# The short set's mLSTM as full-length scores: one round for each query chunk in place of a chunk recurrence in two directions

## The chip, the cores and the metric

One NeuronCore of a Trainium2 chip runs the whole program. The metric is the device time of one execution in microseconds; the kernel before takes 2311.3 us, the median of three runs (2310.19 to 2314.37).

## The reference

One encoder layer runs on two token sets with the same weights: `x_prompt` with 1024 tokens (set A, "long") and `x_sample` with 512 tokens (set B, "short"), 1024 channels each. After a norm and one big input projection there are two branches, an mLSTM in both directions (4 heads of 256) and a dilated attention (3 groups of 8 heads of 64); both are gated, projected and merged. The change touches the mLSTM of the short set. In one direction the reference computes, chunk by chunk of 128 positions,

```python
bc = jnp.cumsum(fc, axis=-1)
d_log = jnp.where(tril, bc[..., :, None] - bc[..., None, :] + ic[..., None, :], -jnp.inf)
a = bc + m[..., None]
mt = jnp.maximum(a, jnp.max(d_log, axis=-1))
sc = jnp.einsum('nhtk,nhsk->nhts', qc, kc) * jnp.exp(d_log - mt[..., None])
wa = jnp.exp(a - mt)
num = jnp.einsum('nhts,nhsv->nhtv', sc, vc) + wa[..., None] * jnp.einsum('nhtk,nhkv->nhtv', qc, c_mat)
den = jnp.sum(sc, axis=-1) + wa * jnp.einsum('nhtk,nhk->nht', qc, n_vec)
h = num / jnp.maximum(jnp.abs(den), jnp.exp(-mt))[..., None]
...
c_new = decay[..., None, None] * c_mat + jnp.einsum('nhsk,nhsv->nhkv', kw, vc)
```

and then sums both directions and normalises each head. Without chunks the same `h_t` is a sum over all earlier positions s of `(q_t . k_s) * exp(u_s - M_t) * v_s`, where `u` is the input gate less the running sum `bc` of log forget gates and `M_t` the running maximum of `u` (at least 0); the divisor is the larger of the weights' own sum in absolute value and `exp(-(bc_t + M_t))`.

## The kernel before, in words

TensorE's and SP's instructions stand in the order in which the program is written (`manual_schedule`); for VectorE, ScalarE and GpSimd a scheduler sets the order. Every product that must be exact runs as three passes over pieces split in two (`mm3`, lines L193 to L195: high x high, high x low, low x high); plain 128x128 products of unsplit numbers appear twice each in the records.

After the long set's input projection the program is a row of stages, each made of small dependent steps with dense work strewn between: the long set's scans (`mlstm(A)`), its attention (`attend(A)`), the short set's scans (`mlstm(B)`), its attention, the ends. The dense work is the `Fill` object's list of units: `fill.stage(steps, shares)` spreads a fixed number of steps over the stage (`STEPS`, 194 for the short set's scans), and `fill(1/3)` issues what is due. A step is three 512-wide products in a row (`dense`). Weights for them come by `wraw` DMAs (L241) and are split by ScalarE (L249) and VectorE (L250); a unit's end is written out by ScalarE and VectorE (L713, L714). Beside the short set's scans runs `combine(A)`, the mixing of the long set's attention groups, one piece after each half round: VectorE mostly (L1412 to L1419), with a turn on TensorE (L1424).

The gates: `gates_of` puts the gate columns into the tile `gall`, and `lanes` (L841 to L926) turns them so that head, direction and chunk are lanes, scans along 128 positions (L870, L873), carries the maximum across chunks, and writes the rows `rw` and the columns `col`. For the short set this runs in pieces beside `attend(A)`.

`mlstm` has a round for each head, chunk and direction: 32 for the short set. Once a head, `prepare` makes k.q for equal chunks (L987) and turns k (L996) with ScalarE copies (L989, L997). `front(k)`, one round ahead, masks and exponentiates the row (L1019, L1021), multiplies it with the scores (L1022), splits it into `sch` and `scl` (L1025, L1026), weights and splits q (L1030 to L1034) and k (L1040, L1041). `core(k)` then issues the products: scores by v into the PSUM tile `num`, k by v into `kv`, q by the carried state `C` into `num`; updates and splits the state (L1072 to L1079); and divides (L1082 to L1086, L1089). In the second half of a head's rounds the two directions meet, and the chain to `hn` follows: square and sum (L1091), a root on GpSimd (L1092, L1093), scaling (L1094). Three rounds later `turn` transposes `hn` into an `a` tile (L1101), VectorE multiplies the gate (L1103) and SP stores it. PSUM holds two banks of `a`, two of `num`, two of `kv`, and two of the dense work.

Of the kernel before, what the change touches and what calls it, by code (L numbers as in the profile page):

```python
# [37 lines left out]
EPS = 1e-6  # L38
NEG = -1e30
# [32 lines left out]
class Tokens:  # L72


    def __init__(self, dram, S, x, y, name):
        self.S, self.x, self.y, self.n, self.nblk, self.name = S, x, y, S // P, S // BLK, name
        t = lambda shape, what, dt=F32: dram.tile(shape, dt, name=f"{what}_{name}")
        self.qk = t([16, P, S], "qk")
        self.vs = t([2, S, D], "vs")
        self.G = t([8, P, S], "G")  # L80
        self.aqk = t([2, 24, P, S], "aqk")
        self.av = t([S, 1536], "av")
        self.az = t([4, P, S], "az")
        self.gt = t([2, 8, P, S], "gt")
        self.rw = t([8, self.n, 2, P], "rw")
        self.ym = t([12, P, S], "ym")
        self.og = t([3, 4, S, OW], "og")

# [88 lines left out]
class Net:  # L177
# [651 lines left out]

    def gates_of(self, T, t):  # L830

        return T.gall.rearrange("p (j r) -> p j r", r=32)[:, :, :4 * T.n].rearrange("p j (h c) -> p j h c", c=T.n)[:, :, :, t]

    def gate_tile(self, T, pool):
        T.gall = pool.tile([P, P], F32, name=f"gall{T.S}")
        self.nc.gpsimd.memset(T.gall, 0.0)
        T.col = pool.tile([P, 3, 64], F32, name=f"col{T.S}")
        T.gb = pool.tile([P, 1], F32, name=f"gb{T.S}")
        self.nc.sync.dma_start(T.gb, self.a[f"gb{T.n}"])

    def lanes(self, T, sb, bank):  # L841

# [109 lines left out]
    def mlstm(self, T, fill, steps, first, banks, lead, after, beside=()):  # L952
# [10 lines left out]
        with ExitStack() as stack:  # L963
# [184 lines left out]
                next(beside, None)  # L1148
            self.flush(lambda p: True)


    def att_load(self, T, u):

# [474 lines left out]
STEPS = (310, 232, 194, 290, 86)  # L1628


def body(tc, a):
    N = Net(tc, a)
    nc = tc.nc
    (x1, y1), (x2, y2) = a["runs"]
    with ExitStack() as st:
        st.enter_context(tc.manual_schedule(engines={mybir.EngineType.PE}))
        pool = lambda name, bufs, **kw: st.enter_context(tc.tile_pool(name=name, bufs=bufs, side="left", **kw))
# [3 lines left out]
        B = Tokens(dram, 512, a[x2], a[y2], "b")  # L1641
# [5 lines left out]
        ps = N.pool(sps, "ps", 8, "left", PSUM)  # L1647
        with ExitStack() as s1:
# [128 lines left out]
        with ExitStack() as s1:  # L1777
            s1.enter_context(tc.manual_schedule(engines={mybir.EngineType.PE, mybir.EngineType.SP}))
            N.defer = True
            ring = N.pool(s1, "ring", 1, "left")  # L1780
            N.wraw = [ring.tile([P, RING], F32, name=f"wraw{i}") for i in range(2)]
            N.wsplit = [[ring.tile([P, RING], F32R, name=f"w{x}{i}") for x in "hl"] for i in range(3)]
            N.arena = N.pool(s1, "arena", 1, "left")
            N.gate_tile(B, N.pool(s1, "gates", 1, "left"))
            short = N.short_units(B)
            N.last = (B, 0)
            finals = [N.final(*x) for x in ((A, 0), (A, 1), (B, 0))]
            units = short[:-4] + N.branches(A, 0, 0, short[-4:])
# [12 lines left out]
            keep.close()  # L1801
            kept = {}

            def hold(name, make):
                def go():
                    kept[name] = make()
                return go

            with ExitStack() as s2:
                sp = N.pool(s1, "sp", 1, "right")  # L1810
                N.sw = Rot(N, [sp.tile([P, BLK], F32R, name=f"sw{i}") for i in range(4)])
                sraw = sp.tile([P, BLK + 2], F32R, name="sraw")
                N.sg, N.sraw = Rot(N, [sraw[:, :BLK]]), sraw.bitcast(F32)
                N.mlstm(A, fill, STEPS[0], N.ml_load(A, 0), ("a", "num", "kv"), 4,
                        hold("qkv", lambda: N.att_load(A, 0)))
                with ExitStack() as s3:
                    lanes = N.lanes(B, N.pool(s3, "lane2", 1, "right"), lambda: N.bank("o").rearrange("p a b -> p (a b)"))
# [24 lines left out]
            end = N.pool(s1, "end", 1, "right")  # L1842
            N.xo_bufs.insert(0, ("late", [end.tile([P, BLK], F32, name=f"xo2{i}") for i in range(2)]))
            with ExitStack() as s2:
                cmb_ps = N.pool(s2, "cmb_ps", 2, "right", PSUM)
                azs = [end.tile([P, BLK], F32, name=f"az{i}") for i in range(2)]
                mixed = N.combine(B, lambda: cmb_ps.tile([P, 4, P], F32, name="tp2"), ("V0a", "V1a"),
                                  ("X1", "Q0"), N.osb, azs, False)
                next(mixed)
                fill.stage(STEPS[4], 3 * B.n + 6)  # L1850
                fill(4)
                for _ in mixed:
                    N.tick()
                    fill(1)
                N.flush(lambda p: True)
            while fill.step():
                if fill.done % 8 == 0:
                    N.tick()
            N.flush(lambda p: True)


def _layout(i):

    f = lambda n: np.asarray(i[n])
    w = f("w_in")[0]
# [13 lines left out]
    def gate_bias(n):  # L1879
        o = np.zeros((4, 32), np.float32)  # L1880
        o[:, :4 * n] = np.repeat(gb, n, axis=1)
        return o.reshape(P, 1)
# [9 lines left out]
        "gb8": gate_bias(8), "gb4": gate_bias(4),  # L1892
# [22 lines left out]
```

## Time and profile before

| What | Value |
|---|---|
| Time, median of 3 runs | 2311.3 us |
| Span of the profiled execution | 2308.8 us |
| TensorE busy | 2261.8 us (98%) |
| VectorE, ScalarE, GpSimd busy | 1493.6, 1134.9, 663.0 us |
| Mean DMA rate | 181 GB/s |
| Mean granted TensorE clock | 0.995 |

The profiled execution is one of its own: its span, from the first instruction to the last, is 2.5 us below the median time. In rows of instructions, `out<-in` gives the tiles, then partitions x elements, a count, the busy time in us and the mean of one in ns, and the idle time ahead with what ended it. In rows of the timeline the start and the length are in us, and the idle time ahead stands in brackets. TensorE's records overlap, so the pace is read from the starts of neighbours.

### The profile page before, as it was taken

The numbers are of one execution on the slowest core, as the hardware profiler recorded it, in microseconds if no ns is written. First come the engines' busy times: TensorE is split into PE (matmuls) and PEld (weight loads), VectorE is DVE, ScalarE is ACT, GpSimd is POOL, SyncE is SP. The second block draws the span as 40 slices with busy tenths as digits, with TensorE's granted clock in tenths as the row PEclk, the third lists the DMA queues.
The fourth block names the chain that finished last, engine by engine and source line by source line (L and its number), as shares of the span: only waits on it lengthen the run. The fifth ranks groups of instructions, "written<-read, shape, count | busy, mean of one in ns | idle before, by whom it ended". The sixth has DMA issues, their size and how long they took to land.

```text
span 2308.8 us, 36431 instructions
## 1 busy us (share of the span) xinstructions
PE 2261.8 (98%) x12610; PEld 1977.8 (86%) x12610; DVE 1493.6 (65%) x2905; ACT 1134.9 (49%) x2375; POOL 663.0 (29%) x888
## 2 busy tenths in 40 slices
PE   8999999999999999999999999999999999999998
PEld 8999888888788888889999889998878788888787
DVE  7765577689886654466777756665488844555563
ACT  6332243434444443366667656766666544544432
POOL 2000333333332232135556500011144321421321
PEclk9999999999999999999999999999999999999999
DMA  3652455542222243294674689887678778686673
GB/s 120 169 127 74 171 207 193 192 171 103 108 104 86 84 151 114 78 331 129 217 241 146 189 219 234 230 237 207 190 252 252 216 229 242 198 254 208 214 257 113
DMA packets 253170, 418.85 MB, mean 181 GB/s; under 512 B 25177, under 2 KB 150297, under 8 KB 252986
## 3 DMA queue, kind: packets, MB, share of 16 engines
q1 hardware_dynamic: 249384, 403.93, 55.9%
q10 hardware_dynamic: 3602, 12.59, 1.4%
q8 instruction: 100, 1.64, 0.3%
q14 instruction: 84, 0.69, 0.1%
HBM read 296.44 MB, written 128.39 MB: 184 GB/s over the span
## 4 chain that ended last, share of the span: by engine, by line
PE 78%; DMA 8%; DVE 5%; issue 5%; ACT 2%; SPq 1%; POOL 1%; DVEq 0%; POOLq 0%; ACTq 0%
PE d L195 11%; PE d L193 11%; PE d L194 11%; PE dense L193 10%; PE dense L195 10%; PE dense L194 10%; PE o L1296 3%; PE pt L1284 2%; PE lg L1261 2%; PE num L193 1%; DVE pwk L678 1%; PE num L195 1%; PE num L194 1%; DMA vs_a<-vz 1%; DMA Q<-aqk_b 1%
## 5 line engine op out<-in xcount | busy, mean ns | idle before, releaser
L193 PE MATMUL dense<-H,wh 128*128 128x512 f32 x672 | 279.5, 416 | 1.4 <-DVE sw L714 1.4
L195 PE MATMUL dense<-H,wl 128*128 128x512 f32 x672 | 265.7, 395 | 0.0
L194 PE MATMUL dense<-H,wh 128*128 128x512 f32 x672 | 265.5, 395 | 0.0
L195 PE MATMUL d<-Hh,phla 128*128 128x512 f32 x608 | 237.1, 390 | 3.8 <-DVE phla L610 3.8
L193 PE MATMUL d<-Hh,phla 128*128 128x512 f32 x608 | 236.6, 389 | 0.0
L194 PE MATMUL d<-Hl,phla 128*128 128x512 f32 x608 | 236.5, 389 | 0.0
L250 DVE TENSOR_TENSOR wl<-wraw,wh 128x1024 fp32r<-128x1024 f32 (+1 forms) x130 | 163.0, 1254 | 98.2 <-ACT wh L249 96.5
L1273 DVE CUSTOM_DVE_ANT_0 ls<-lg,bias 128x256 f32<-128x256 f32 (+1 forms) x288 | 93.7, 362 | 145.6 <-PE lg L1261 55.9
L1277 ACT ACTIVATE ls<-ls,nm 128x256 f32<-128x256 f32 (+1 forms) x288 | 130.0, 453 | 97.6 <-DVE nm L1275 79.4
L195 PE MATMUL d<-Hh,phlb 128*128 128x512 f32 x456 | 177.4, 389 | 0.0
L193 PE MATMUL d<-Hh,phlb 128*128 128x512 f32 x456 | 177.4, 389 | 0.0
L194 PE MATMUL d<-Hl,phlb 128*128 128x512 f32 x456 | 177.4, 389 | 0.0
L249 ACT ACTIVATE wh<-wraw 128x1024 fp32r<-128x1024 f32 (+1 forms) x130 | 137.0, 1054 | 80.1 <-PE dense L194 41.4
L628 POOL TENSOR_TENSOR psum_w<-pw_raw 128x512 f32<-128x512 f32 x38 | 59.2, 1557 | 376.2 <-DMA pw_raw<-w_in 353.0
L195 PEld LDWEIGHTS dense<-H,wl 128*128 128x128 f32 x672 | 127.7, 190 | 29.0
L193 PEld LDWEIGHTS dense<-H,wh 128*128 128x128 f32 x672 | 128.2, 191 | 18.3 <-issue 1.8
L194 PEld LDWEIGHTS dense<-H,wh 128*128 128x128 f32 x672 | 128.5, 191 | 16.6
L193 PE MATMUL d<-vhi,Hh 128*128 128x322 f32 x448 | 141.1, 315 | 1.3 <-ACT Hh L353 1.1
L194 PE MATMUL d<-vlo,Hh 128*128 128x322 f32 x448 | 139.8, 312 | 2.2 <-DVE vlo L427 2.2
L195 PE MATMUL d<-vhi,Hl 128*128 128x322 f32 x448 | 140.3, 313 | 0.4 <-DVE Hl L354 0.2
L195 PEld LDWEIGHTS d<-Hh,phla 128*128 128x128 f32 x608 | 114.1, 188 | 29.4 <-DVE phla L610 5.9
L194 PEld LDWEIGHTS d<-Hl,phla 128*128 128x128 f32 x608 | 114.1, 188 | 23.8
(552 smaller groups left out, 6206.9 us busy)
## 6 DMA issues: line engine op xcount, KB each, us to landing
pw_raw<-w_in SPq DMA_DIRECT2D x76, 512.0 KB
wraw<-w_in SPq DMA_DIRECT2D x76, 512.0 KB
aqk_a<-pwk SPq DMA_DIRECT2D x48, 512.0 KB
aqk_b<-sw SPq DMA_DIRECT2D x48, 256.0 KB
wraw<-w_pm SPq DMA_DIRECT2D x24, 512.0 KB
wraw<-w_out SPq DMA_DIRECT2D x24, 512.0 KB
wraw<-w_v SPq DMA_DIRECT2D x18, 512.0 KB
erep<-erow SPq DMA_DIRECT2D x16, 512.0 KB
```

Source lines behind the costliest of these rows:

```text
L193: nc.tensor.matmul(out, lh, rh, start=start, stop=False)
L194: nc.tensor.matmul(out, lh, rl, start=False, stop=False)
L195: nc.tensor.matmul(out, ll, rh, start=False, stop=stop)
L249: self.splits = (nc.scalar.activation(hi[:, :n], raw[:, :n], AF.Copy), nc.vector.tensor_sub(lo[:, :n], raw[:, :n], hi[:, :n].bitcast(F32)))
L250: nc.vector.tensor_sub(lo[:, :n], raw[:, :n], hi[:, :n].bitcast(F32)))
L628: self.nc.gpsimd.tensor_add(s[:, 0], ws[1][:, 0], ws[1][:, 1])
L678: nc.vector.scalar_tensor_tensor(y, raw[:, i:i + S], cw[:, i:i + 1], y, op0=OP.mult, op1=OP.add)
L1261: nc.tensor.matmul(lg[:, hh, c:c + w], q[hh][:, qs], z[:, k0:k0 + w], start=z is k[hh], stop=z is not k[hh])
L1273: nc.vector.tensor_tensor_reduce(out=ls[:, hh], in0=ts["lg"][hh], in1=bt[:, hh], scale=1.0, scalar=NEG, op0=OP.add, op1=OP.max, accum_out= ...
L1277: nc.scalar.activation(ls[:, hh], ls[:, hh], AF.Exp, bias=nm[:, hh:hh + 1], accum_out=ot[:, 128 + hh:129 + hh])
L1284: nc.tensor.transpose(pp[:, hh * nk + x], ts["ls"][:, hh, x * P:(x + 1) * P], self.ident)
L1296: nc.tensor.matmul(po[:, hh * 64:hh * 64 + 64], pt[:, hh * nk + x], v[:, kt[x], c0 + hh * 64:c0 + hh * 64 + 64], start=x == 0, stop=x == n ...
```

## The change

For the short set alone (512 tokens) there are a new `lanes_short` and a new `mlstm_short`.

- `gall` holds the four chunks apart (128 x 4 x 128), so that a lane is a head and direction alone and a scan runs along all 512 positions (L1181, L1185). No maximum is carried across chunks. It writes one row of maxima for each lane to `rw` and, by four transposes, the columns `u` and `exp(-(bc + M))` to `col`.
- `mlstm_short` has 16 rounds, one for each head and query chunk i. `weigh(k)` makes the weights for both directions in one tile of five blocks: the i+1 blocks of key chunks 0 to i for the forward one, the 4-i blocks of chunks i to 3 for the backward one. VectorE subtracts the row of maxima from the columns (two instructions), GpSimd masks the two diagonal blocks, ScalarE takes the exponential.
- `front(k)` makes the scores of query chunk i with all four key chunks (eight 128x128 products, L1262), VectorE multiplies the weights with them (L1264, L1265), ScalarE and GpSimd split the result (L1268, L1269).
- `core(k, d)` adds up the scores by v over the direction's blocks in one `num` bank and divides; the second direction adds to the first, and the chain to `hn` follows. `turn` comes one round later. There is no `kv`, no state and no turned k; `num` has four banks. The buffer of G is doubled, the rows are fetched once a head and direction.
- The number of dense steps in the stage stays 194. The scratch of DMAs issued by GpSimd goes to 1024 bytes.

```diff
+        for q, o in ((0, li), (64, lf)):
+            nc.scalar.activation(o[0:32], p[q:q + 32], AF.Identity, bias=T.gb[q:q + 32])
...
+        nc.vector.tensor_tensor_scan(bc, one, lf, 0.0, op0=OP.mult, op1=OP.add)
+        yield
+        nc.vector.tensor_sub(u, li, bc)
+        nc.gpsimd.memset(one, 0.0)
+        nc.vector.tensor_tensor_scan(cm, one, u, 0.0, op0=OP.add, op1=OP.max)
+        nc.vector.tensor_add(bc, bc, cm)
...
+            bank = {"a": lambda: ps.tile([P, 4, P], F32, name="a"),
+                    "num": lambda: ps.tile([P, 512], F32, name="num", bufs=4)}
...
+            def weigh(k):
+                h, i = rounds[k]
+                w = made[k] = sb.tile([P, n + 1, P], F32, name="rm")
+                for d in range(2):
+                    b0, c0, m = (0, 0, i + 1) if d == 0 else (i + 1, i, n - i)
+                    u = T.col[:, c0:c0 + m, 32 * d + h]
+                    row = ms[h, d][:, i * P:(i + 1) * P]
+                    nc.vector.tensor_tensor(w[:, b0:b0 + m], u[:, :, None].to_broadcast([P, m, P]),
+                                            row[:, None, :].to_broadcast([P, m, P]), op=OP.subtract)
+                    sg = 1 if d == 0 else -1
+                    nc.gpsimd.affine_select(out=w[:, i + d], in_=w[:, i + d], pattern=[[sg, P]], compare_op=OP.is_ge, fill=NEG,
+                                            base=0, channel_multiplier=-sg)
+                nc.scalar.activation(w, w, AF.Exp)
+
+            def front(k):
...
+                p = psum("a")
+                for j in range(n):
+                    for ct in range(2):
+                        nc.tensor.matmul(p[:, j], kk[:, ct, j * P:(j + 1) * P], q[:, ct, i * P:(i + 1) * P], start=ct == 0,
+                                         stop=ct == 1)
+                nc.vector.tensor_mul(w[:, :i + 1], w[:, :i + 1], p[:, :i + 1])
+                nc.vector.tensor_mul(w[:, i + 1:], w[:, i + 1:], p[:, i:])
...
+                nc.scalar.activation(sch, w, AF.Copy)
+                nc.gpsimd.tensor_sub(scl, w, sch.bitcast(F32))
...
+            def core(k, d):
...
+                js = list(range(i + 1) if d == 0 else range(i, n))
+                pn = psum("num")
+                for j in js:
+                    self.mm3(pn[:, :258], (sch[:, j + d], scl[:, j + d]), (v[0][:, j], v[1][:, j]), j == js[0], j == js[-1])
...
+                if k + 1 < len(rounds):
+                    front(k + 1)
+                if k + 2 < len(rounds):
+                    weigh(k + 2)
+                fill(2 / 3)
+                core(k, 0)
+                fill(1 / 3)
+                next(beside, None)
+                self.tick()
+                turns.pop(k - 1, lambda: None)()
+                fill(2 / 3)
+                core(k, 1)
+                fill(1 / 3)
+                next(beside, None)
...
-                    N.mlstm(B, fill, STEPS[2], kept["head"], ("kv", "num", "a"), 1,
+                    N.mlstm_short(B, fill, STEPS[2], kept["head"], ("num", "a"), 1,
...
-    nc = _bacc.Bacc("TRN2", target_bir_lowering=False, num_devices=1)
+    nc = _bacc.Bacc("TRN2", target_bir_lowering=False, num_devices=1, dynamic_dma_scratch_size=1024)
```

How the order changes. TensorE in a round of the short set's scans before: the state's product, dense work, then q by the carried state (`ch`, `cl` are its split halves).

```order
L195 MATMUL kv<-V1a,kl 128x258
L193 MATMUL dense<-H_7784,wh_7757 128x512
L194 MATMUL dense<-H_7785,wh_7757 128x512
L195 MATMUL dense<-H_7784,wl_7758 128x512
L193 MATMUL num<-ch_17672,qh 128x258
L194 MATMUL num<-cl_17673,qh 128x258
L195 MATMUL num<-ch_17672,ql 128x258
```

TensorE now, where a round begins: one group of eight score products into an `a` bank, then dense work.

```order
L1262 MATMUL a<-Q_17374 128x128 x8
L193 MATMUL dense<-H_7784,wh_7755 128x512
L194 MATMUL dense<-H_7785,wh_7755 128x512
L195 MATMUL dense<-H_7784,wl_7756 128x512
L193 MATMUL dense<-H_7786,wh_7755 128x512
L194 MATMUL dense<-H_7787,wh_7755 128x512
L195 MATMUL dense<-H_7786,wl_7756 128x512
```

The `kv` and `num<-ch` products are gone from the short set's stage, and the score group stands once a round instead of once a head. VectorE before, in the same stage (`cf`, `cl`: the state and its low half; `kl`: the weighted k; `cw`, `az`: the combine; `sw`, `wl`: dense work):

```order
L1426 TENSOR_TENSOR az_16697<-a,az_16697 128x512
L1084 RECIPROCAL r<-r 128x1
L1079 TENSOR_TENSOR cl_17755<-cf_17422,ch_17754 128x516
L1089 SCALAR_TENSOR_TENSOR X_16719<-num,r,X_16719 128x256
L1041 SCALAR_TENSOR_TENSOR kl<-Q_17439,col_7767,kh 128x256
L250 TENSOR_TENSOR wl_7756<-wraw_7752,wh_7755 128x1024
L1394 TENSOR_TENSOR cw_17855<-V1b 128x8
L1075 SCALAR_TENSOR_TENSOR cf_17501<-cf_17501,rw_16712,kv 128x516
L714 SCALAR_TENSOR_TENSOR sw_7867<-dense,sw_7866 128x128x4
L1022 TENSOR_TENSOR rm<-rm,st_16707 128x128
```

VectorE now, with the weights of a later round (L1246), the combine's sums (L1620, L1621), a division (L1285 to L1291) and the product with the scores (L1264, L1265):

```order
L1246 TENSOR_TENSOR rm<-col_7767,rw_16681 128x512
L1246 TENSOR_TENSOR rm<-col_7767,rw_16682 128x128
L250 TENSOR_TENSOR wl_7758<-wraw_7752,wh_7757 128x1024
L1620 TENSOR_TENSOR K_16720<-K_16720 128x512
L714 SCALAR_TENSOR_TENSOR sw_7867<-dense,sw_7866 128x128x4
L1285 TENSOR_SCALAR r<-num,col_7767 128x1
L1621 TENSOR_TENSOR K_16720<-K_16720 128x512
L1286 SCALAR_TENSOR_TENSOR r<-num,r 128x1
L1287 RECIPROCAL r<-r 128x1
L1291 SCALAR_TENSOR_TENSOR hs<-num,r,hs 128x256
L1264 TENSOR_TENSOR rm<-rm,a 128x384
L1265 TENSOR_TENSOR rm<-rm,a 128x256
```

The four state and k instructions have left the row, and the subtraction and the product of five blocks have come in; the division still stands behind the same combine and dense rows.

More of the change, by code (lines that the diff above doesn't have):

```diff
@@ L84, in __init__ @@
         self.gt = t([2, 8, P, S], "gt")
-        self.rw = t([8, self.n, 2, P], "rw")
+        self.rw = t([8, S] if S == BLK else [8, self.n, 2, P], "rw")
         self.ym = t([12, P, S], "ym")
@@ L830, in gates_of @@
     def gates_of(self, T, t):
+        if T.S == BLK:
+            return T.gall[:, t].rearrange("p (j r) -> p j r", r=32)[:, :, :4]
         return T.gall.rearrange("p (j r) -> p j r", r=32)[:, :, :4 * T.n].rearrange("p j (h c) -> p j h c", c=T.n)[:, :, :, t]
     def gate_tile(self, T, pool):
-        T.gall = pool.tile([P, P], F32, name=f"gall{T.S}")
+        short = T.S == BLK
+        T.gall = pool.tile([P, 4, P] if short else [P, P], F32, name=f"gall{T.S}")
         self.nc.gpsimd.memset(T.gall, 0.0)
-        T.col = pool.tile([P, 3, 64], F32, name=f"col{T.S}")
+        T.col = pool.tile([P, 4, P] if short else [P, 3, 64], F32, name=f"col{T.S}")
         T.gb = pool.tile([P, 1], F32, name=f"gb{T.S}")
-        self.nc.sync.dma_start(T.gb, self.a[f"gb{T.n}"])
+        self.nc.sync.dma_start(T.gb, self.a["gb1" if short else f"gb{T.n}"])
     def lanes(self, T, sb, bank):
@@ L1146, in mlstm, with lanes_short @@
                 fill(1)
+                turns[k]()
+                next(beside, None)
+            self.flush(lambda p: True)
+    def lanes_short(self, T, sb, bank):
+        nc = self.nc
+        L = 64
+        t = lambda what, rows=L: sb.tile([rows, BLK], F32, name="l_" + what, bufs=1)
+        li, lf, e, u1, l = (t(x) for x in ("li", "lf", "e", "u1", "l"))
+        p = bank()
+        for c in range(4):
+            nc.tensor.transpose(p[:, c * P:(c + 1) * P], T.gall[:, c], self.ident)
+        for q, o in ((0, li), (64, lf)):
+            nc.scalar.activation(o[0:32], p[q:q + 32], AF.Identity, bias=T.gb[q:q + 32])
+            nc.scalar.activation(o[32:64][:, ::-1], p[q + 32:q + 64], AF.Identity, bias=T.gb[q + 32:q + 64])
+        yield
+        nc.scalar.activation(e, lf, AF.Abs)
+        nc.scalar.activation(e, e, AF.Exp, scale=-1.0)
+        nc.vector.tensor_scalar(u1, e, 1.0, None, op0=OP.add)
+        nc.scalar.activation(l, u1, AF.Ln)
+        nc.vector.scalar_tensor_tensor(u1, u1, 1.0, e, op0=OP.subtract, op1=OP.subtract)
+        yield
+        nc.scalar.activation(e, l, AF.Exp, scale=-1.0)
+        nc.vector.tensor_mul(e, e, u1)
+        nc.vector.tensor_sub(l, l, e)
+        nc.vector.scalar_tensor_tensor(lf, lf, 0.0, l, op0=OP.min, op1=OP.subtract)
+        one = t("one")
+        nc.gpsimd.memset(one, 1.0)
+        bc, cm, u = u1, l, li
+        nc.vector.tensor_tensor_scan(bc, one, lf, 0.0, op0=OP.mult, op1=OP.add)
+        yield
+        nc.vector.tensor_sub(u, li, bc)
+        nc.gpsimd.memset(one, 0.0)
+        nc.vector.tensor_tensor_scan(cm, one, u, 0.0, op0=OP.add, op1=OP.max)
+        nc.vector.tensor_add(bc, bc, cm)
+        yield
+        q1, mn = t("q1", P), lf
+        nat = lambda d, x, o=0: x[o:o + 32] if d == 0 else x[o + 32:o + 64, ::-1]
+        for d in range(2):
+            s = slice(32 * d, 32 * d + 32)
+            nc.vector.tensor_copy(nat(d, q1), u[s])
+            nc.scalar.activation(nat(d, q1, 64), bc[s], AF.Exp, scale=-1.0)
+            nc.vector.tensor_copy(nat(d, mn), cm[s])
+            self.put(("rw", T.S), T.rw[4 * d:4 * d + 4], mn[32 * d:32 * d + 4], mn)
+        yield
+        p = bank()
+        for c in range(4):
+            nc.tensor.transpose(p[:, c * P:(c + 1) * P], q1[:, c * P:(c + 1) * P], self.ident)
+        nc.vector.tensor_copy(T.col.rearrange("p q r -> p (q r)"), p)
+        yield
@@ L1816, in body @@
                 with ExitStack() as s3:
-                    lanes = N.lanes(B, N.pool(s3, "lane2", 1, "right"), lambda: N.bank("o").rearrange("p a b -> p (a b)"))
+                    lanes = N.lanes_short(B, N.pool(s3, "lane2", 1, "right"), lambda: N.bank("o").rearrange("p a b -> p (a b)"))
                     N.attend(A, fill, STEPS[1], kept["qkv"], ("pt", "o", "lg"), 10, hold("head", lambda: N.ml_load(B, 0)),
@@ L1891, in _layout @@
         "conv": np.concatenate([f("m_conv_w")[0], f("m_conv_b")], 0).reshape(4, 16, P).transpose(2, 1, 0),
-        "gb8": gate_bias(8), "gb4": gate_bias(4),
+        "gb8": gate_bias(8), "gb1": gate_bias(1),
         "hnw": f("m_head_norm_w")[0].reshape(8, P).T,
```

91 lines of the change are left out of this document (added).

## The prediction

> **What bounds the kernel now.** I read the page's head first, then the windows over the short set's scan stage, then TensorE's waits in it, then single rows of its timeline. The profiled execution spans 2308.8 us; the median of the runs is 2311.3 us, so a span of mine becomes a time by adding 2.5 us.
>
> ```profile
> span 2308.8 us, 36431 instructions
> ...
> 1480.00:1600.00 120.00, 120.00 (x782) 108.24 (x782) 70.55 (x265) 84.04 (x259) 14.25 (x22) 1.00 0.81 219
> 1649.40:1700.00 50.60, 49.99 (x287) 43.26 (x286) 36.87 (x86) 31.35 (x73) 25.22 (x39) 1.00 0.78 249
> 1700.00:1750.00 50.00, 45.41 (x254) 39.61 (x253) 42.24 (x99) 30.34 (x67) 21.75 (x41) 0.93 0.78 243
> 1750.00:1800.00 50.00, 45.84 (x260) 39.70 (x259) 42.67 (x99) 29.63 (x68) 22.50 (x40) 0.97 0.77 240
> 1800.00:1850.00 50.00, 45.21 (x244) 38.58 (x243) 41.94 (x100) 27.37 (x59) 18.69 (x32) 0.97 0.68 204
> 1850.00:1871.50 21.50, 21.50 (x104) 17.77 (x103) 8.34 (x10) 6.66 (x11) 2.33 (x5) 1.00 0.56 183
> ```
>
> In the windows the columns after the length are busy us of TensorE, weight loads, VectorE, ScalarE and GpSimd, then the granted clock. The first row lies in the long set's attention, where the short set's lanes run: TensorE has no gap at all. The other five are the short set's scans, 1649.4 to 1871.5. TensorE is idle there for 0.6 + 4.6 + 4.2 + 4.8 = 14.2 us, and the granted clock is 0.93, 0.97 and 0.97 in the three middle windows: 3.5 + 1.5 + 1.5 = 6.5 us of full clock not granted, of which I take 6, since a little of it falls into the idle time. VectorE is busy 172.1 of 222.1 us, 84% in the middle. So this stage is TensorE's own work plus some 20 us of holes. What ends the holes:
>
> ```profile
> PE num L193 <- issue: 5.7, 2, 4.6
> PE num L193 <- ACT X L1086: 5.2, 2, 3.0
> PE a L1101 <- ACT hn L1094: 2.5, 1, 2.5
> ...
> 1776.79 0.39 PE L195 MATMUL dense<-H,wl 128*128 128x512 f32 x1
> 1780.18 0.39 PE L193 MATMUL num<-V0a,sch 128*128 128x258 f32 x1 [3.00 <-ACT X L1086]
> ...
> 1781.57 0.56 PE L194 MATMUL dense<-H,wh 128*128 128x512 f32 x1
> ...
> 1784.51 0.63 PE L195 MATMUL dense<-H,wl 128*128 128x512 f32 x1
> 1784.93 0.45 PE L193 MATMUL dense<-H,wh 128*128 128x512 f32 x1
> ```
>
> 10.9 us are a `num` product that waits for its accumulator: there are two banks, and VectorE and ScalarE have not drained the one before (the row of 3.00 us: ScalarE's read of it ended just then). The row put down to "issue" has the same place. 2.5 us are a turn of `hn` that came too soon. After the 3.00 us gap, from 1781.6 to 1784.9, the products run at half pace, 0.42 us for 512 columns instead of 0.23 (below): the gap is paid a second time in clock.
>
> **TensorE's work.** The order counts 144 products of 258 columns fewer (384 to 240), 32 transposes of k fewer, and 96 score products of 128x128 more (32 to 128). All 594 dense products stay. Paces, as starts of neighbours:
>
> ```profile
> 1656.14 0.60 PE L996 MATMUL a<-ident,Q 128*128 128x128 f32 x4
> 1656.49 0.48 PE L193 MATMUL dense<-H,wh 128*128 128x512 f32 x1
> 1656.81 0.40 PE L194 MATMUL dense<-H,wh 128*128 128x512 f32 x1
> 1657.04 0.40 PE L195 MATMUL dense<-H,wl 128*128 128x512 f32 x1
> ...
> 1700.98 0.28 PE L194 MATMUL num<-cl,qh 128*128 128x258 f32 x1
> 1701.10 0.28 PE L195 MATMUL num<-ch,ql 128*128 128x258 f32 x1
> ...
> 1773.86 1.95 PE L987 MATMUL a<-Q 128*128 128x128 f32 x16
> 1775.56 0.48 PE L193 MATMUL dense<-H,wh 128*128 128x512 f32 x1
> 1775.88 0.40 PE L194 MATMUL dense<-H,wh 128*128 128x512 f32 x1
> ```
>
> A 258-wide product takes 0.12 us. Eight score products (16 records, two each) take 1.70 us and lengthen the next dense product from 0.23 to 0.32: 1.79 us, or 0.224 each. Four transposes take 0.35 + 0.09 = 0.44, 0.11 each. So 96 x 0.224 = +21.5, 144 x 0.12 = -17.3, 32 x 0.11 = -3.5: together +0.7 us. The recurrence that goes was cheap in TensorE's reduced-precision form, and the scores that come are in the slow one, so by its own work TensorE gains nothing. The lanes' transposes (6 small ones before, 8 now) cancel within 0.3 us. What the change can win is in the 20 us of holes.
>
> **VectorE.** It loses the k weighting, the state update and its splitting and the 32 small products; it gains, per round, a subtraction and a product over 640 columns, each in two instructions.
>
> ```profile
> L1079 DVE TENSOR_TENSOR cl<-cf,ch 128x516 fp32r<-128x516 f32 x24 | 18.2, 760 | 0.5 <-ACT ch L1078 0.4
> L1041 DVE SCALAR_TENSOR_TENSOR kl<-Q,col,kh 128x256 fp32r<-128x256 f32 x24 | 12.3, 514 | 0.1
> L1075 DVE SCALAR_TENSOR_TENSOR cf<-cf,rw,kv 128x516 f32<-128x516 f32 x16 | 11.9, 745 | 3.7 <-PE kv L195 3.7
> L1022 DVE TENSOR_TENSOR rm<-rm,st 128x128 f32<-128x128 f32 x32 | 11.7, 369 | 13.1 <-ACT st L989 6.9 <-ACT rm L1021 6.2
> L1419 DVE TENSOR_TENSOR K<-K 128x512 f32<-128x512 f32 x8 | 6.0, 748 | 0.0
> L1426 DVE TENSOR_TENSOR az<-a,az 128x512 f32<-128x512 f32 x4 | 2.8, 690 | 1.6 <-PE a L1424 1.5
> ```
>
> Away go 18.2 + 12.3 + 11.9 + 11.7 = 54.1 us. The subtraction is priced by L1419 (both sources in SBUF, 748 ns for 512), the product by L1426 (one source in PSUM, 690): 640/512 x 1.44 = 1.8 us a round, with two instruction starts more some 2.0; 16 rounds make 29 to 34. VectorE sinks from 172 to about 149 us in a stage of some 208: from 77% to 72%. It stays bursty, because the long set's combine runs beside it as before. ScalarE and GpSimd also lose more than they gain.
>
> **The holes, one by one.** There are now four `num` banks, and a round uses two. Between two uses of a bank lie the products of three others, some one and a half rounds or over 15 us (16 rounds in about 200 us), where only one lay between before, some half round; the drains were late by at most 4.6 us. I take all 10.9 us as gone, and the 0.8 us that the waits leave of the 14.2. What stays is the turn of `hn`. In the new order 21 dense, eight score and six `num` products stand between the last product of a round and its turn: 21 x 0.23 + 1.79 + 6 x 0.12 = 7.3 us. The chain that must fit in is VectorE, ScalarE, GpSimd twice, ScalarE. Its longest here:
>
> ```profile
> 1792.44 0.28 PE L195 MATMUL num<-ch,ql 128*128 128x258 f32 x1
> ...
> 1799.48 2.42 DVE L1412 TENSOR_TENSOR K<-V1b,cw 128x512 f32<-128x512 f32 x3
> ...
> 1802.35 0.51 ACT L1094 ACTIVATE hn<-X,r 128x256 f32<-128x256 f32 x1 [2.45 <-POOL r L1093]
> ...
> 1802.91 0.33 PE L1101 MATMUL a<-ident,hn 128*128 128x128 f32 x1 [2.51 <-ACT hn L1094]
> ```
>
> From 1792.72 to 1802.86, 10.1 us, in a place that left 7.7 (1802.91 less 2.51 less 1792.72). So the room is about what it was, and 2.5 us over the whole stage was its price. If chains stay as long as here the new turns lose up to 2.8 us each time; if they shorten with ScalarE's and GpSimd's load, nothing. I take one to two late turns, 3 us, and one clock window behind them, 1.7 us (half of the 3.3 us of half pace above), and 0.5 us where a turn of the combine and of `hn` follow each other on two `a` banks: 5.2 us, between 0 and 18 (four turns as late as that one, each with its clock window).
>
> The Trainium skill, "TensorE: Matmul & The Clock Gate", Part 1 (the HAM clock gate), says that the clock halves after an idle window of about 3.4 us. By that rule the new gaps of under 3 us would cost no clock and the time would be 1.7 us lower; the trace halves it after 3.00 us, and I go by the trace.
>
> **The ends of the stage.** The first `num` product now needs rows of `rw`, two subtractions, the mask, the exponential, the product, the rounding and a GpSimd remainder of 640 columns.
>
> ```profile
> L1019 POOL TENSOR_SCALAR_AFFINE_SELECT rm<-rw x11: 291/292/628, 1654.1 to 1698.6; 128x128 f32<-128x128 f32 x11
> L628 POOL TENSOR_TENSOR psum_w<-pw_raw 128x512 f32<-128x512 f32 x38 | 59.2, 1557 | 376.2 <-DMA pw_raw<-w_in 353.0
> L870 DVE TENSOR_TENSOR_SCAN l_u<-l_one,l_lf 64x128 f32<-64x128 f32 x1 | 0.4, 406 | 0.0
> ```
>
> The rows are there at 1654.1, and SP issues them from the same place. The remainder is 640/512 x 1.557 = 1.95 us and the rest some 4.5: ready near 1660.6. TensorE passes 2.67 shares of 5.4 dense steps (14.4 x 0.69 = 9.9 us) and two score groups (3.6 us) from 1649.4 before it asks, near 1662.9. Cost 0, at worst 3 us. The lanes' scans are four times as wide: 1.6 us each by L870, in pieces that hold VectorE for up to 3 us in the attention, which shows no TensorE gap in 120 us; cost 0, at worst 3 us with the cover gone. The smaller DMA scratch concerns GpSimd's DMAs, of which the kernel issues none: 0. Eight broadcast fetches of rows replace sixteen on SP, and the wait for a row buffer's readers goes; what stood behind it (weight fetches) can only come sooner.
>
> **Sum.** -14.2 - 6 + 0.7 + 5.2 = -14.3 us on the profiled execution: 2294.5, so a time of 2297.0 us.
>
> **The rivals.** First, half of the holes come back: bursts remain. GpSimd's remainder is now one instruction of 1.95 us in place of shorter ones, and VectorE can wait behind it:
>
> ```profile
> 1703.80 0.83 POOL L1034 TENSOR_TENSOR ql<-qw,qh 128x256 fp32r<-128x256 f32 x1 [0.82 <-ACT qh L1033]
> 1703.98 1.21 DVE L1418 TENSOR_TENSOR K<-K 128x512 f32<-128x512 f32 x1
> ...
> 1801.83 0.68 DVE L1418 TENSOR_TENSOR K<-K 128x512 f32<-128x512 f32 x1
> ```
>
> The same sum of 512 columns took 1.21 us beside a GpSimd instruction and 0.68 without: it waited 0.53. With 1.95 + 2 x 0.29 = 2.5 us of GpSimd a round wholly added to VectorE, 149 + 40 = 189 us would still be below TensorE's 203 (222.1 - 20.2 + 0.7), but bursts would reach the turns. Then half of 14 us returns: 2304 us, chance 0.17. The Trainium skill, "SBUF — State Buffer", section "SBUF: two separate sides", calls this an exclusive lock on a shared port pair; by that rule, which the two rows bear out, the wait is a whole instruction at most, as just reckoned.
>
> Second, slower: the turn decides. With room for 7.3 us, a chain of 10.2 costs 2.9 us and 1.7 us of clock, 4.6 a time. TensorE's saving of 19.5 us without new stalls is eaten once it happens in more than four of 16 rounds; in eight rounds it is 37 us, and the time 2329 us. Against it: the room was 7.7 us before, and one turn waited. Chance 0.11.
>
> Third, no change: the lanes, the start and the late turns together take the 14 us, each near its worst (3 + 3 + 8 more): 2309 us, chance 0.08. That the change does not do what it says is excluded by the counts above. My forecast has 0.64, its own range 2291 to 2302.
>
> **How the numbers follow.** A measurement of this kernel tells about 0.2%, 4.6 us, from no change. Faster: 0.64 + 0.16 of the half case = 0.80. Same: 0.08 and the rest of the half case, 0.09. Slower: 0.11. The range runs from 2290 (all holes gone) to 2309.
>
> **What would show it.** Right: the stage near 208 us instead of 222, `num` no longer in TensorE's waits, granted clock near 1.00, a dense-to-`num` order without gaps; left over, small waits of `a` for `hn`. The new VectorE rows at 1.0 us a pair and a score group of 1.70 us confirm the terms. Wrong: `a` waiting for `hn` in many rounds with clock under 0.95, `num` waiting for `scl`, or new gaps near 1490 to 1590.

## The result, and the profile after

The changed kernel took 2292.3 us (median of 4 runs, 2291.0 to 2293.1) beside 2312.8 us (median of 4, 2310.2 to 2315.8) for the kernel before: ratio 0.9913, 95% interval 0.9892 to 0.9935. That is 20.6 us less. The forecast was 14.3 us less, 2297.0. The profiled execution spans 2290.3 us, 18.5 less than before.

The windows of the changed kernel, with the columns as in the prediction (the last two, after the clock, are the busy share of the DMA engines and their GB/s): first the same stretch of the long set's attention, then the short set's scans, now from 1647.5 to 1851.5, then ten microseconds in the short set's attention.

```profile
1480.00:1600.00 120.00, 119.73 (x772) 107.32 (x771) 71.61 (x251) 85.11 (x253) 16.27 (x23) 1.00 0.80 221
1647.50:1700.00 52.50, 50.82 (x292) 43.90 (x291) 37.98 (x86) 23.86 (x40) 14.85 (x23) 1.00 0.84 257
1700.00:1750.00 50.00, 50.00 (x293) 43.66 (x292) 37.34 (x94) 24.78 (x40) 14.88 (x30) 1.00 0.82 255
1750.00:1800.00 50.00, 49.96 (x296) 43.64 (x295) 40.07 (x102) 22.85 (x42) 13.38 (x22) 1.00 0.83 255
1800.00:1851.50 51.50, 51.50 (x283) 44.25 (x282) 31.18 (x70) 20.95 (x36) 8.83 (x13) 1.00 0.63 185
...
1890.00:1900.00 10.00, 9.52 (x33) 7.89 (x33) 3.78 (x8) 3.73 (x6) 2.32 (x2) 0.51 0.98 304
```

The scans take 204.0 us instead of 222.1. TensorE's idle time there fell from 14.2 to 1.7 us (first column, 52.50 less 50.82, and almost nothing later), and the clock is 1.00 throughout. The trace of before spent 13.7 us of this stage at half clock, 1.4 us of them idle; half of the other 12.3 us, 6.1 us, was lost to the clock, and that is gone too. 12.5 + 6.1 = 18.6 us of holes went and the stage is 18.1 us shorter, so TensorE's own work grew by some 0.5 us. What TensorE still waits for in the stage, in us, times, longest:

```profile
PE a L1303 <- ACT hn L1296: 0.8, 1, 0.8
PE num L195 <- POOL scl L1269: 0.5, 1, 0.5
PE dense L193 <- DVE sraw L690: 0.4, 1, 0.4
```

Against the three rows of before: no `num` product waits for a bank, one turn of `hn` waits 0.8 us instead of 2.5, and one `num` product waits 0.5 us for `scl`, the low halves of its weighted scores. The new work itself, first a score group in TensorE's row, then groups of VectorE (L250, L1614 and L1628, of the dense work and the combine, are for comparison later) and GpSimd:

```profile
1657.09 1.95 PE L1262 MATMUL a<-Q 128*128 128x128 f32 x16
1658.80 0.48 PE L193 MATMUL dense<-H,wh 128*128 128x512 f32 x1
1659.11 0.40 PE L194 MATMUL dense<-H,wh 128*128 128x512 f32 x1
```

```profile
L250 DVE TENSOR_TENSOR wl<-wraw,wh 128x1024 fp32r<-128x1024 f32 x25 | 32.9, 1317 | 23.8 <-ACT wh L249 23.8
L1614 DVE TENSOR_TENSOR K<-V0b,cw 128x512 f32<-128x512 f32 x12 | 8.9, 795 | 0.0
L1628 DVE TENSOR_TENSOR az<-a,az 128x512 f32<-128x512 f32 x4 | 2.7, 687 | 0.7 <-PE a L1626 0.7
L1265 DVE TENSOR_TENSOR rm<-rm,a 128x512 f32<-128x512 f32 (+3 forms) x16 | 7.7, 479 | 0.0
```

```profile
L1269 POOL TENSOR_TENSOR scl<-rm,sch 128x640 fp32r<-128x640 f32 x16 | 25.7, 1604 | 27.1 <-ACT sch L1268 27.1
```

Eight score products take 1.71 us, the remainder 1.60 us. Behind the stage something is given back. In the short set's attention a `K` row, fetched from memory, came late, and half clock followed:

```profile
PE dense L193 <- ACT K L1678: 1.1, 1, 1.1
PE dense L194 <- POOL K L1679: 0.8, 1, 0.8
PE dense L193 <- ACT sw L815: 0.5, 1, 0.5
```

That is 2.4 us of waits near 1888 and 10.2 us at half clock from 1889.6 on (the 0.51 above), some 7 us in all. Stalls that before had outside the scans are gone in exchange, among them two steps of 3.4 us at half clock, so that what lies ahead of the scans is 1.9 us shorter and what lies behind them 1.5 us longer. These 7 us belong to this one execution: the two-bank kernel below has the same program behind the stage, and its trace shows 2.7 us of waits near there and full clock.

### The profile page after: what moved, and what is told of

Read it like the earlier page. It is cut to its first block, busy times and chain, and to the rows that moved or that the text cites. A ratio compares the mean times of both kernels' runs of the same rounds, so it can differ in the third digit from the quotient of the medians.

```text
span 2290.3 us, 36121 instructions
## 1 busy us (share of the span) xinstructions
PE 2258.5 (99%) x12628; PEld 1975.3 (86%) x12628; DVE 1465.7 (64%) x2851; ACT 1102.2 (48%) x2255; POOL 628.6 (27%) x824
## 5 line engine op out<-in xcount | busy, mean ns | idle before, releaser
L250 DVE TENSOR_TENSOR wl<-wraw,wh 128x1024 fp32r<-128x1024 f32 (+1 forms) x130 | 163.9, 1262 | 106.7 <-ACT wh L249 105.4
```

Source lines behind the costliest of these rows:

```text
L250: nc.vector.tensor_sub(lo[:, :n], raw[:, :n], hi[:, :n].bitcast(F32)))
```

## The experiments

Beside these experiments the kernel before took 2308.0 to 2309.6 us; the changed kernel was not run again beside them, and differences to it under some 3 us tell nothing. Four theories stand against each other: A, the waits for `num` went because there are four banks; B, they went because a bank is asked for less often; C, they went because VectorE is relieved; D, what load still costs in the changed kernel it costs at the turns of `hn`. Later comes E, that GpSimd's load counts too.

**Two `num` banks.**

```
-"num": lambda: ps.tile([P, 512], F32, name="num", bufs=4)
+"num": lambda: ps.tile([P, 512], F32, name="num", bufs=2)
```

> The changed kernel with two num banks instead of four; every engine's order stays the same. Theory A (the prediction's step: the waits for num went because there are four banks): TensorE's waits for num come back, 5 to 11 us in the short set's scans, some of them over 2.2 us and paid again in clock; the time rises by 5 to 16 us to 2297 to 2308. Theory B (the waits went because a bank is asked for less often: 32 times instead of 32 plus carried products, evenly spaced): in the trace of the changed kernel a bank was drained 1.2 to 7.9 us after its last product, and the next but one use began 2.3 us or more after that drain in every case; two banks then do, waits for num under 1 us and the time within 2 us of 2292.3.

2290.4 us, ratio 0.9936 (0.9917 to 0.9956). TensorE's waits in the stage:

```profile
PE num L195 <- POOL scl L1269: 0.8, 1, 0.8
PE a L1303 <- ACT hn L1296: 0.7, 1, 0.7
PE dense L193 <- DVE sraw L690: 0.2, 1, 0.2
```

They are close to those of four banks. Theory A, on which the prediction rested, falls for the changed kernel as it is: two banks do as well.

**Before, with less for VectorE.** The low halves of the weighted k and of the state are left out; in the products the high half stands in for them.

```
-nc.vector.scalar_tensor_tensor(kl, kc, wsc, kh.bitcast(F32), op0=OP.mult, op1=OP.subtract)
+kl = kh
...
-nc.vector.tensor_sub(cl, cf, ch.bitcast(F32))
+cl = ch
```

> The kernel before, its recurrence kept, with the low halves of weighted keys and of the carried state left out in the short set (the high half stands twice in the products), so that TensorE's products stay in number and VectorE loses 12.3 + 18.2 = 30.5 us of its 172.1 in the scans, a little more than the change took from it (172.1 to 146.6 in the stage). Theory C (the change gains because VectorE is relieved): the holes of the scans go, 12 to 20 us less, 2293 to 2301. Theories A and B (banks, or how often and how long a bank is held, decide): drains start a little sooner, but num is still asked for 3 to 8 us after the last use but one, half or more of the 14.2 us stay, 0 to 8 us less, 2305 to 2313.

2296.5 us, ratio 0.9952 (0.9936 to 0.9969), 11 to 12 us less than before, where the two-bank kernel beside it had 18 us less. With the recurrence and two banks kept, no `num` product waits any more; what stays in the scans is this:

```profile
PE a L1105 <- ACT hn L1098: 1.7, 1, 1.7
PE kv L193 <- DVE cf L1077: 1.6, 1, 1.6
PE kv L193 <- ACT sraw L698: 0.3, 1, 0.3
```

So the relief of VectorE suffices, in the kernel before, to remove the waits for `num`, and brings some two thirds of the gain: theory C. The products also have no `kl` and `cl` to wait for in this version, but none of TensorE's waits of before named them.

**Scores twice.**

```
-for j in range(n):
+for j in [j for j in range(n) for _ in range(2)]:
     for ct in range(2):
         nc.tensor.matmul(p[:, j], kk[...], q[...], start=ct == 0, stop=ct == 1)
```

> The changed kernel with each of its 128 score products issued twice into the same bank (the second pair starts afresh, so the scores are the same). If TensorE paces the scans of the changed kernel, as all the theories of a hole-free stage say: one group of eight took 1.71 us, so 16 x 1.71 = 27 us more, 2317 to 2322, and little added elsewhere. If another engine paces them or TensorE has slack that the trace hides: under 15 us. The extra time also gives the drains more room, so holes should not grow.

2318.6 us, 28.2 more than the kernel with two banks, measured beside it; 16 x 1.71 = 27.4 were worked out. The scans show no wait of TensorE at all. In the changed kernel TensorE paces this stage, and each microsecond given to it is paid in full.

**Subtraction twice.**

```
+for _ in range(2):
     nc.vector.tensor_tensor(w[:, b0:b0 + m], u[...], row[...], op=OP.subtract)
```

> The changed kernel with its 32 subtractions of weights (0.483 us each) done twice, 15.5 us more of VectorE in the scans: 146.6 + 15.5 = 162 of 204 us, 79%, more than the 77% of before, with the order of the rest as it is. Theory C (VectorE's load made the holes): the holes come back, 8 to 20 us, 2300 to 2312. Theories A and B: the weights have a round's lead, and the drains come at most 0.5 to 1 us later; 0 to 3 us, 2292 to 2295.

2303.3 us, ratio 0.998 (0.9965 to 0.9995): some 11 to 13 us lost (the profiled execution took 2311.3, one of the longest, so its waits are more than a typical one's). Where, in the same view:

```profile
PE a L1304 <- ACT hn L1297: 9.0, 4, 4.8
PE num L195 <- POOL scl L1270: 1.1, 1, 1.1
```

No wait for `num`, but four late turns. C is right that VectorE's load makes holes; the changed kernel shows them at another place.

**The same, with each turn a round later.**

```
-turns.pop(k - 1, lambda: None)()
+turns.pop(k - 2, lambda: None)()
```

The fetch of the next head's gate (`load_G`) moves one round later with it, and each turn left over at the end has half as much dense work ahead of it.

> The kernel with its subtractions done twice, and each turn of hn one round later (the load of the next head's gates moves one round later with it). There the doubled subtraction brought 9.0 us of waits for hn in four turns and about 11 us of time, and no wait for num. Theory D (a heavier VectorE costs time only where something needs its drain soon, and after the change that is the turn): with a round more, some 12 us, for the chain the waits for hn go, 0 to 3 us over the changed kernel, 2290 to 2295. Rival (VectorE at 79% is a bound whatever the order; the stall moves to scl, a or num): the time stays at 2299 to 2306 and the waits have another name.

2293.2 us, ratio 0.994 (0.9924 to 0.9956): 9 to 10 of the 11 to 13 us are back, no turn waits, and 1.7 us for an `a` bank and 1.1 for `scl` remain. Theory D. VectorE is busy for 157.5 of 204 us here, 77%, the share of the kernel before; that is no bound, and it costs time only where its result is wanted soon.

This trace also bears on B. VectorE is as full as before, and still no `num` product waits. Each bank was drained at least 1.0 us before the next group but one began, so two banks would have done as well (worked out from this trace; no run has two banks and the doubled subtraction). A group asks for the bank of the last but one 8.4 us or more after that one's last product in the changed kernel, and 5.1 us or more in the kernel before. So the wider spacing of B can keep the waits for `num` away with VectorE as full as before (GpSimd stays lighter here, 57.6 us against 90.5), as the relief of C does in the kernel before without the spacing.

**Before, with the state's subtraction on GpSimd.**

```
-nc.vector.tensor_sub(cl, cf, ch.bitcast(F32))
+nc.gpsimd.tensor_sub(cl, cf, ch.bitcast(F32))
```

> The kernel before, with only the short set's subtraction for the low half of the carried state moved from VectorE to GpSimd, nothing left out: VectorE loses 18.2 of 172.1 us in the scans, GpSimd gains 24 of about 1.3 us, 31 us over its 90. Theory C (VectorE's load made the holes of before): the share of the gain of the kernel with the lighter VectorE that goes with 18.2 of 30.5 us, 12 x 0.6 = 7 us less than before, ratio 0.995 to 0.999. Rival (GpSimd's longer subtraction comes later on the state's chain, and VectorE shares its port with it): products wait for cl, 0 to 15 us more, ratio 1.000 to 1.0065.

2311.9 us, ratio 1.0013 (1.0002 to 1.0024): no gain. The waits for `num` stay (12.4 us), and none of TensorE's waits names `cl`. The windows over 1649.4 to 1871.5, of the kernel before and of this one, and two groups of this one:

```profile
1649.40:1871.50 222.10, 207.95 (x1141) 178.94 (x1140) 172.06 (x390) 125.34 (x272) 90.49 (x155) 0.97 0.73 229
```

```profile
1649.40:1871.50 222.10, 207.47 (x1138) 177.99 (x1137) 169.97 (x367) 124.94 (x272) 123.86 (x179) 0.97 0.73 229
```

```profile
L1079 POOL TENSOR_TENSOR cl<-cf,ch 128x516 fp32r<-128x516 f32 x24 | 34.3, 1431 | 18.0 <-ACT ch L1078 15.9 <-DMA V0b<-og_a 2.1
L1419 DVE TENSOR_TENSOR K<-K 128x512 f32<-128x512 f32 x8 | 7.9, 987 | 0.0
```

18.2 us of instructions left VectorE and its busy time fell by 2.1: the rest got longer (L1419 from 748 to 987 ns). So this is no case against C; VectorE was not relieved.

**Remainder twice.**

```
+for _ in range(2):
     nc.gpsimd.tensor_sub(scl, w, sch.bitcast(F32))
```

> The changed kernel with GpSimd's remainder of the weighted scores (16 of 1.6 us) done twice: GpSimd goes from 52 to about 78 us in the scans, VectorE's own list stays. In the kernel before, 34.3 us of subtractions put on GpSimd made VectorE's other instructions 16 us longer, so that 18.2 us taken from it left it only 2.1 us lighter. Theory E (a part of the change's gain is GpSimd's own relief, from 90 to 52 us, because VectorE runs faster beside an idle GpSimd): VectorE's busy time in the scans rises by 6 to 12 us with no instruction added, drains and hn come later as with the doubled subtraction, and the time rises by 3 to 10 us, 2295 to 2302. Rival (GpSimd's load does not reach TensorE): 0 to 2 us, the remainder is only 1.6 us later with half a round to spare.

2308.9 us, ratio 0.9995 (0.9983 to 1.0006): 29.5 us more on an engine that was a quarter busy took the whole gain, more than the 10 us that theory E allowed. VectorE's busy time over the whole program rose from 1465.7 to 1479.7 us with no instruction added to it. TensorE's waits, and VectorE's and GpSimd's groups:

```profile
PE a L1304 <- ACT hn L1297: 7.2, 3, 3.6
PE a L1262 <- DVE az L1629: 2.5, 1, 2.5
PE num L195 <- POOL scl L1270: 2.5, 1, 2.5
```

```profile
L1615 DVE TENSOR_TENSOR K<-V0b,cw 128x512 f32<-128x512 f32 x12 | 13.2, 1154 | 0.0
L1629 DVE TENSOR_TENSOR az<-a,az 128x512 f32<-128x512 f32 x4 | 2.7, 684 | 1.2 <-PE a L1627 1.2
L1246 DVE TENSOR_TENSOR rm<-col,rw 128x128 f32<-128x128 f32 (+3 forms) x32 | 14.2, 483 | 13.8 <-POOL scl L1270 7.1 <-DMA rw<-rw_b 6.8
```

```profile
L1270 POOL TENSOR_TENSOR scl<-rm,sch 128x640 fp32r<-128x640 f32 x32 | 55.2, 1726 | 30.1 <-ACT sch L1268 29.0
```

L1615 (L1614 in the changed kernel), whose sources lie in SBUF, went from 795 to 1154 ns: its shortest took 676 ns, and its longest, which ran beside a remainder, 2058. L1629 (L1628), one of whose sources lies in PSUM, stayed at 684, though two of its four ran beside a remainder from end to end. One late turn, in the timeline:

```profile
1804.25 0.19 POOL L1295 TENSOR_SCALAR r<-r 128x1 f32<-128x1 f32 x1
1804.52 1.53 POOL L1270 TENSOR_TENSOR scl<-rm,sch 128x640 fp32r<-128x640 f32 x1
...
1806.01 0.55 POOL L1296 TENSOR_TENSOR r<-r,mhalf 128x1 f32<-128x1 f32 x1
1806.08 0.89 DVE L1246 TENSOR_TENSOR rm<-col,rw 128x384 f32<-128x384 f32 x2 [3.47 <-POOL scl L1270]
1806.59 0.51 ACT L1297 ACTIVATE hn<-hs,r 128x256 f32<-128x256 f32 x1 [1.55 <-POOL r L1296]
```

Here the second subtraction stands between GpSimd's two steps of the root for `hn`, and VectorE waits 3.47 us for the buffer of weights that this subtraction still reads. So GpSimd's load reaches the turn in three ways: longer instructions on VectorE, its own queue, and buffers held longer. This run does not part them.

**The same, with each turn a round later** (the edit above).

> The kernel with GpSimd's remainder done twice (which took some 16 us, all the gain: 7.2 us of waits for hn, 2.5 for a, 2.5 for scl, and half clock four times), and each turn of hn one round later. There the chain from the last num product to hn grew from 4.90 to 6.18 us on average, 0.9 us of that before VectorE's sum and 0.3 us on GpSimd. Theory D (as for VectorE: what costs is the turn, which comes too soon for a later hn): the waits for hn go, 6 to 12 us less, 2296 to 2303; what stays is a and scl. Theory D in full (everything follows the turn): 2290 to 2295. Rival (GpSimd's load holds the stage elsewhere, and a later turn only renames it): 2304 to 2310.

2301.2 us, ratio 0.9968 (0.9956 to 0.998): 6 to 8 of some 17 us came back, as D said of the turns. The waits for `hn` are gone; 4.4 us for `a`, 2.2 for `scl` and 2.8 of dense products for VectorE stay. GpSimd's load costs elsewhere too.

**Before, with less for GpSimd.** The low half of the weighted queries is left out, the high half standing in for it.

```
-nc.gpsimd.tensor_sub(ql, qw, qh.bitcast(F32))
+ql = qh
```

> The kernel before with the low half of the weighted queries left out in the short set (the high half stands twice in the products): GpSimd loses 22.3 of its 90.5 us in the scans, VectorE's list and TensorE's products stay. Theory E (GpSimd's load makes VectorE's drains late through what they share): VectorE's instructions shorten by 5 to 10 us in sum, the waits for num shrink by half or more, 5 to 12 us less, 2296 to 2304, ratio 0.9948 to 0.998. Rival (only VectorE's own list counts, as when 30.5 us were left out of it): VectorE's busy time and the num waits stay, ratio 0.998 to 1.001.

2306.4 us, ratio 0.999 (0.9978 to 1.0001). The waits for `num` fell from 10.9 to 7.2 us and VectorE's busy time from 172.1 to 168.3, but the time is not told from before's. For the kernel before, VectorE's own list counts more than GpSimd's load; E is borne out in the waits there and not in the time.

**Versions meant to be faster.** The rows for the branch projections two steps ahead of their use; then that with the late turn; then that with the output norm's weight loaded some 100 us later.

```
-            for k in range(5):
+            for k in range(6):
...
-                if k:
+                if k > 1:
```

> The changed kernel with the rows for the branch projections fetched two steps ahead of their rounding instead of one. In the changed kernel a row issued at 1879.9 landed at 1887.6, and TensorE waited 1.1 + 0.8 + 0.5 us for its halves and then ran 10.2 us at half clock. If that late row is what was given back behind the stage: the gap near 1888 goes and with it 2.4 us and up to 5 us of clock, 2285 to 2290. If the gap comes from the burst of loads whatever the lead: no change, 2290 to 2294.

> The same with each turn of hn one round later as well. The changed kernel has one wait for hn left, 0.8 to 1.0 us, and spare of 0.05 us in two rounds. If turns with so little room cost time in runs other than the profiled one: 1 to 4 us less than with the rows alone and a narrower spread, 2283 to 2289. If not, within 1 us of it.

> The changed kernel with the rows fetched two steps ahead and the 512 KB of the output norm's weight loaded some 100 us later, out of the burst in which the short set's attention begins (the DMA engines are over 0.9 busy there, and its first use is at 1993.5). With the rows ahead alone the gap near 1888 had gone, but a wait of 2.5 us for a load came at 1894. If the burst as a whole makes these loads late: 512 KB are about 2 us at the 260 to 280 GB/s of the burst, the wait shrinks to 0 to 1 us, 1 to 4 us less than the changed kernel, 2287 to 2291. If the loads come late by their order in the queues: no change, 2291 to 2294.

2293.0, 2293.4 and 2294.5 us (ratios 0.9936, 0.9934 and 0.9927): none is told from the changed kernel. In the trace with the rows ahead, the wait near 1888 went, and another load was waited for a few microseconds on:

```profile
PE lg L1463 <- DMA ymr<-ym_a: 2.5, 1, 2.5
PE lg L1463 <- DMA V0a<-aqk_b: 0.2, 1, 0.2
```

With the norm's weight out of the way the wait at that place is 2.8 us, so its 512 KB do not explain it. The two-bank kernel, whose rows are as they were, waits 1.4 us for the same load; that the rows ahead moved the wait is thus not shown, and why a load comes late there stays open.

## Why the prediction was right, point by point

- **The stage and its 20 us of holes**: right, and it is the whole result; 18.6 us of them went, and doubling the scores showed that TensorE paces what is left.
- **TensorE's own work, +0.7 us**: some 0.5 by the balance above. The score group of 1.70 us measured 1.71.
- **All 10.9 us of `num` waits go**: right in size, by luck in the reason put first. "There are now four `num` banks" is not it: two do as well. In the changed kernel a bank is drained 1.2 to 7.8 us after its last product, 3.2 on average, and the next use but one begins at least 2.3 us after that; in the kernel before the drain took up to 11.4 us, 5.2 on average. The groups follow each other more evenly, and the drains come sooner; the doubled subtraction with the late turn suggests that the first is enough, and the lighter kernel before shows that the second can be.
- **VectorE from 172 to 149 us**: 146.6, with 29.7 us added (29 to 34 were reckoned). This term was worked out and then given no share in the gain. The lighter kernel before shows that such relief can remove the waits for `num` by itself, the doubled subtraction that it keeps the turns of `hn` in time.
- **"ScalarE and GpSimd also lose more than they gain"**: true (GpSimd from 90 to 52 us) and priced at nothing. The kernel with the remainder twice shows what that relief guards: with GpSimd back at 88 us the gain is gone. The first rival, bursts that reach the turns through GpSimd, names a mechanism that this kernel shows; in the changed kernel GpSimd's load was some 30 us too small for it.
- **New stalls, 5.2 us**: the term that was mis-sized. They were 1.7 us without half clock. The chain to `hn` took 8.7 us at its longest and 5.3 on average from the last `num` product; the forecast took one or two as long as the 10.1 us of before. These 3.5 us, with 0.1 us more of half clock gone than the 6 reckoned and 0.2 us less work, are the 3.8 us by which the stage beat its forecast of 207.8.
- **The ends of the stage, cost 0**: right. One `num` product waited 0.5 us, and TensorE was idle for 0.3 us of the 120 beside the lanes.
- **What the prediction did not have**: the late row near 1888, some 7 us, balanced in this trace by stalls of before that did not come back. That the time outside the scans came out as forecast, at no change, is luck in this one execution.

The holes of before thus come from drains that a full VectorE makes late for banks that are asked for soon. That VectorE's list decides there is shown by taking from it; adding to it in the changed kernel brings no wait for `num` back, but late turns. How much of the 18 us each of relief, spacing and GpSimd's lighter load brought is not parted: the changed kernel has all three.

## What to carry to other kernels

When TensorE waits for an accumulator, look at what delays the drain, and at how soon the bank is asked for again, before adding banks: here two banks did what four were credited with. Work moved from VectorE to GpSimd can come back as longer instructions on VectorE, as it did here. Where TensorE waits for a result, asking for it one round later can hide a heavier producer: it gave back 9 to 10 us of 11 to 13 here, and in the changed kernel, where hardly a turn was late, the version with it showed neither gain nor cost.

## What the runs showed of the hardware

Moving 18.2 us of subtractions from VectorE to GpSimd lightened VectorE by 2.1 us, and there they took 34.3. Beside a busier GpSimd, VectorE's sums of two SBUF sources got longer (L1615, 795 to 1154 ns on average, 676 for its shortest and 2058 beside a remainder), and one with a source in PSUM did not (L1629, 687 to 684). The Trainium skill, "SBUF — State Buffer", section "SBUF: two separate sides", has an exclusive lock on a shared port pair for the first kind; these rows agree. The subtraction of weights (L1246, both sources in SBUF) kept its 483 ns, but none of its 32 runs fell beside a remainder, which reads the buffer that it must wait for.

Half clock lies on a grid. In the clock records of the 14 traces, all intervals at half clock begin at multiples of 3.413 us from each other within a trace and last one, two or three such steps, apart from the one that the program's end cuts off. Of the steps at full clock, those in which TensorE was idle for over 54% were all followed by half clock, those under 40% by none, and between the two both occurred (39 such falls, the program's end not counted, against over 9200 steps without). So what a gap costs depends on where it falls: in before, a gap of 2.51 us near 1800 that lay across two steps cost no clock, and one of 2.22 us near 1826 inside one step cost 3.4 us at half speed. The Trainium skill, "TensorE: Matmul & The Clock Gate", Part 1 (the HAM clock gate), has the free-running window of 3413 ns, and the traces agree; it asks for an idle window, and here half of one was enough.
